# A gate table laid out by expert blocks in DRAM, five row buffers, and block 0's expert rows fetched after block 1's

## The chip, the cores and the metric

The kernel runs on one core of one Trainium2 chip. The metric is the device time of one execution in microseconds (us). The core has five engines with a program each: TensorE (PE in the profile; its weight loads are shown as PEld), VectorE (DVE), ScalarE (ACT), GpSimd (POOL) and SyncE (SP). Each works through its own program in order and waits on semaphores for the others. Sixteen DMA engines serve the transfers that SP, ACT and POOL issue.

## The reference, cut to what matters

One decoder layer on 512 tokens of width 1024: attention in sixteen heads, then a PEER feed-forward layer, in which every token picks 16 of 16384 single-neuron experts for each of 8 heads. All the work that the change touches is in the second half:

```python
def peer_ffn(xn, wq, subkeys, u_table, v_table):       # u_table, v_table: (16384, 1024)
    q = (xc @ wq).reshape(PEER_CHUNK, PEER_HEADS, 2, PEER_HALF)
    s = jnp.einsum('chpd,hpkd->chpk', q, subkeys)
    s1, i1 = lax.top_k(s[:, :, 0], PEER_TOPK)          # 16 of 128 keys
    s2, i2 = lax.top_k(s[:, :, 1], PEER_TOPK)
    cs, ci = lax.top_k(cand, PEER_TOPK)                # cand: the 256 sums s1 + s2
    eidx = jnp.take_along_axis(cidx, ci, axis=-1)      # cidx: i1 * 128 + i2
    g = jax.nn.softmax(cs, axis=-1)
    ug = jnp.take(u_table, eidx, axis=0)
    vg = jnp.take(v_table, eidx, axis=0)
    hid = jnp.einsum('cd,chkd->chk', xc, ug)
    a = jax.nn.gelu(hid, approximate=False) * g
    return jnp.einsum('chk,chkd->cd', a, vg)
```

## The kernel before, in words

The 512 tokens are four blocks of 128 (TB = 4, P = 128). The kernel handles the experts of these blocks in two ways.

**Block 0 and the first 32 tokens of block 1 fetch rows.** `gathers()` goes through 256 slots: 128 picks of block 0 from the table u, then the same picks from v. `issue(n)` takes a buffer `row` from the pool `rowp` and has POOL fetch one row of 4 KB for each of the 128 partitions (L504). For u, DVE forms the dot product of the rows with the tokens (L513, called a dot below); for v it adds the rows times their weights to `acc` (L520). `gatherq()` does the same for the first 32 tokens of block 1, spread over the 128 partitions, in 32 slots of u alone (fetch L723, dot L731). Both take their buffers from `rowp`, and a fetch into a buffer waits for the DVE instruction that used what was in it.

**The other 352 tokens (DH) are computed densely.** For each of 64 pairs of expert blocks (NPAIR; a pair is 256 experts), TensorE multiplies a 1 MB piece of u (`wraw`, split by ACT and DVE into a high part `whi` and a low part `wlo`, L126 and L127) with all 352 tokens, and ACT applies the Gelu (L534). The first 34 pairs (SPILL) are done early, and their results (`hs`) are parked in DRAM (`Hd`); the other 30 are done in the last stage. There, each pair's hidden values `ga` are multiplied on DVE (L863) by the gate table `gt`, split into `ah` (ACT, L126) and `al` (DVE, L127), and multiplied on TensorE with a 1 MB piece of v (`vr`, split into `vh` and `vl`) into six PSUM accumulators (`oa`, L886).

**The gate table** holds for each expert and token the weight of that pick, mostly zero. It is built between these two, from one-hot matrices (DVE writes `o` and `og` at L768 to L774, TensorE multiplies them into `pg`, L796; ACT copies `pg` into `gs`, L786), in 12 groups of 32 tokens (NG = 12, GT = 32), and stored in the DRAM tensor `Gd` (L788, 2 MB for each group). It is read back as `gt` in pieces of two pairs (four expert blocks, 768 KB, L835).

So there are three stages that matter here. The stage of the tables (about 480 to 780 us) interleaves table building, parked pairs (`spill`) and row fetches: `merge` mixes generators of the program by their weights, and a scheduler then orders each engine's instructions. The last stage (about 800 to 1575 us) interleaves `dense()` with `gathers()`; DVE's order there is the order of the program. Between them the gate table must have landed in `Gd` before the first `gt` can be read. In the lines of the profile `row<-in_u_dram,eq` is a fetch for block 1, and `eidx` marks one for block 0.

In the kernel before, two slots of `gathers()` (D_GATHER = 2) are taken into the stage of the tables. The generator keeps three fetches ahead of the slot that it is at, and `rowp` has four buffers.

Of the kernel before, what the change touches and what calls it, by code (L numbers as in the profile page):

```python
# [10 lines left out]
F32 = mybir.dt.float32  # L11
# [6 lines left out]
ALU = mybir.AluOpType  # L18
# [3 lines left out]
P = 128  # L22
T = 512
D = 1024
# [6 lines left out]
HK = NHEAD * TOPK  # L31
NKEY = 128
DT = T - P
GT = 32
# [8 lines left out]
NB = 8  # L43
NG = DT // GT
GS = 2.0 ** 15
NPAIR = NKEY // 2
ET = mybir.EngineType
HP = 100
GF = 1.01
SPILL = 34  # L50
D0_SPILL = 4
D1_SPILL = 4
RF = 1.04
RAWB = 2
HB = 3
SLOPES = [2.0 ** (-8.0 * (h + 1) / NH) for h in range(NH)]
D_GATHER = 2
CA, CB = 4, 12
NCAND = CA * TOPK + CB * 4

# [1 line left out]
def merge(*streams):  # L62

    live = [[0.0, total, gen] for gen, total in streams]
    while live:
        s = min(live, key=lambda e: e[0] / e[1])
        try:
            s[0] += next(s[2])
        except StopIteration:
            live.remove(s)  # L70
# [3 lines left out]
def tile_kernel(ctx: ExitStack, tc: tile.TileContext, x, w_in, w_f, b_f, w_out, wq, skT, u, v, uT, g1, g2, g2r, gfr,  # L74
                cident, ciota, ciota16, cmask, cdist, cmult, csel, out):
    nc = tc.nc

    def pool(name, bufs=1, space=None, stack=ctx):
        kw = {"space": space} if space is not None else {}
        return stack.enter_context(tc.tile_pool(name=name, bufs=bufs, reuse_waits="tile", **kw))  # L80

    gdram = pool("gdram", space=bass.MemoryType.DRAM)
    Gd = gdram.tile([NG, P, NKEY * GT], F32, name="Gd")
    hres = gdram.tile([T, D], F32, name="hres")
    xqd = gdram.tile([GT, D], F32, name="xqd")
    Hd = [gdram.tile([P, 2, DH], F32, name=f"Hd{n}") for n in range(SPILL)]
# [143 lines left out]
    while fresh or stored:  # L230
        n = fresh.pop(0) if fresh and (not stored or (nf - len(fresh)) * ns <= (ns - len(stored)) * nf) else stored.pop(0)
# [3 lines left out]
    with ExitStack() as st:  # L235
# [14 lines left out]
        with ExitStack() as s1:  # L250
# [16 lines left out]
            feed = Feed(wst, items)  # L267
# [3 lines left out]
            for b0 in range(0, TB, 2):  # L271
                nc.scalar.activation(junk[0], xs[b0 // 2][:, 0, :], AF.Square, accum_out=ss[:, b0:b0 + 1])
                sums = nc.vector.tensor_tensor_reduce(out=junk[1], in0=xs[b0 // 2][:, 1, :], in1=xs[b0 // 2][:, 1, :], scale=1.0, scalar=0.0,
                                               op0=ALU.mult, op1=ALU.add, accum_out=ss[:, b0 + 1:b0 + 2])
                _, _, norm1 = normed(xt, xp, xs[b0 // 2], b0, ss[:, b0:b0 + 2], g1c, "n1", feed.start if b0 else None)
# [182 lines left out]
        for c in range(D // WC):  # L458
# [4 lines left out]
            for b in range(0, TB, 2):  # L463
# [9 lines left out]
                if c == D // WC - 1:  # L473
                    ss = small.tile([P, 2], F32, name="n2ss")
                    nc.vector.tensor_reduce(ss, sq[:, b:b + 2, :], axis=AX.X, op=ALU.add)
                    rs, norm2, _ = normed(xt, hp, hb, b, ss, g2t, "n2")
# [8 lines left out]
            nc.sync.dma_start(hres[2 * b * P:2 * (b + 1) * P, :].rearrange("(b p) d -> p b d", p=P), h2[b])  # L485


    rowp = pool("rowp", bufs=4)
    accp = pool("accp")
    acc = accp.tile([P, D], F32, name="acc")  # L490
    hid0 = accp.tile([P, HK], F32, name="hid0")
    a0 = accp.tile([P, HK], F32, name="a0")
    nc.gpsimd.memset(acc, 0.0)


    def gathers():
        rows = {}
        slots = [(u, k) for k in range(HK)] + [(v, k) for k in range(HK)]

        def issue(n):  # L500
            if n < len(slots):
                tab, k = slots[n]
                rows[n] = rowp.tile([P, D], F32, name="row")
                nc.gpsimd.indirect_dma_start(out=rows[n], out_offset=None, in_=tab,  # L504
                                             in_offset=bass.IndirectOffsetOnAxis(ap=eidx[:, k:k + 1], axis=0))

        for n in range(3):
            issue(n)
        for n, (tab, k) in enumerate(slots):
            issue(n + 3)  # L510
            t = rows.pop(n)
            if tab is u:
                nc.vector.tensor_tensor_reduce(out=t, in0=t, in1=xn0, scale=1.0, scalar=0.0, op0=ALU.mult,  # L513
                                               op1=ALU.add, accum_out=hid0[:, k:k + 1])
                if k % TOPK == TOPK - 1:
                    sl = slice(k - TOPK + 1, k + 1)
                    nc.scalar.activation(a0[:, sl], hid0[:, sl], AF.Gelu)
                    nc.vector.tensor_mul(a0[:, sl], a0[:, sl], g0[:, sl])
            else:
                nc.vector.scalar_tensor_tensor(acc, t, a0[:, k:k + 1], acc, op0=ALU.mult, op1=ALU.add)  # L520
            yield 1.0

    def take(gen, n):
        for _ in range(n):
            try:
                yield next(gen)
            except StopIteration:
                return


    def hidden(uu, c, out_):
# [4 lines left out]
    with ExitStack() as st:  # L536
# [5 lines left out]
        NS = P // GT  # L542
# [11 lines left out]
        def spill(fd, n0, n1):  # L554
            for n in range(n0, n1):
                uu = fd.get()
                hs = hsp.tile([P, 2, DH], F32, name="hs")
                for c in range(2):
                    hidden(uu, c, hs[:, c, :])
                    yield 1.0  # L560
                nc.scalar.dma_start(Hd[n], hs)
# [54 lines left out]
        with ExitStack() as s2:  # L616
# [99 lines left out]
            def gatherq():  # L716

                rows = {}

                def issue(k):  # L720
                    if k < HK // NS:
                        rows[k] = rowp.tile([P, D], F32, name="row")
                        nc.gpsimd.indirect_dma_start(out=rows[k], out_offset=None, in_=u,  # L723
                                                     in_offset=bass.IndirectOffsetOnAxis(ap=eq4[:, k:k + 1], axis=0))

                for k in range(3):
                    issue(k)
                for k in range(HK // NS):
                    issue(k + 3)
                    t = rows.pop(k)  # L730
                    nc.vector.tensor_tensor_reduce(out=t, in0=t, in1=xnq, scale=1.0, scalar=0.0, op0=ALU.mult,  # L731
                                                   op1=ALU.add, accum_out=hq4[:, k:k + 1])
                    yield 1.0
# [22 lines left out]
            tab, work = {}, []  # L756
# [21 lines left out]
            def advance():  # L778
                if len(work) > 2 or (work and work[0][4]):
                    tok, scale, _, _, pgs, _ = work.pop(0)  # L780
                    g = tok // GT
                    if tok % GT == 0:
                        tab[g] = gsp.tile([P, NKEY, GT], F32, name="gs")
                    for n, pg in enumerate(pgs):
                        q0 = tok % GT + 4 * n
                        nc.scalar.activation(tab[g][:, :, q0:q0 + 4].rearrange("p i t -> p t i"), pg, AF.Copy, scale=scale)  # L786
                    if tok % GT == GT - NB:
                        nc.sync.dma_start(Gd[g], tab.pop(g).rearrange("p i t -> p (i t)"))  # L788
                for w in work[:-1] if len(work) > 1 else work:
                    if w[4] is None:  # L790
                        w[4] = []
                        for t4 in range(0, NB, 4):
                            pg = pgt.tile([P, 4, NKEY], F32, name="pg")
                            for tt in range(4):
                                for n in range(w[5]):
                                    nc.tensor.matmul(pg[:, tt, :], w[2][:, t4 + tt, :], w[3][n][:, t4 + tt, :], start=(n == 0), stop=(n == w[5] - 1))  # L796
                            w[4].append(pg)
                yield 2.8

            def gates3():  # L800
                yield from tables(1)
                for b in range(2, TB):
                    yield from pairs(b)
                    yield from tables(b)
                yield from tableq()
                while work:
                    yield from advance()

            L2 = 12.8 + 4.0 + 1.5 + 7.4
            merge((pairs(0), L2), (spill(feed, 0, D0_SPILL), 2.0 * D0_SPILL))  # L810
            n1 = D0_SPILL + D1_SPILL
            merge((pairs(1), L2 + 2.0), (spill(feed, D0_SPILL, n1), 2.0 * D1_SPILL))

            ga = gathers()
            merge((gates3(), RF * (2 * L2 + 7.0 + 3 * 2.8 * P // NB)), (spill(feed, n1, SPILL), 2.0 * (SPILL - n1)), (gatherq(), 1.2 * HK / NS),
                  (take(ga, D_GATHER), float(D_GATHER)))

    with ExitStack() as st:
        ep = pool("ep", bufs=2, stack=st)
# [8 lines left out]
        def load_v(i):  # L828
            if i < NPAIR:
                n = seq[i]  # L830
                raws[i] = vr = vrp.tile([P, 2, D], F32, name="vr")
                nc.sync.dma_start(vr, v[2 * n * P:2 * (n + 1) * P, :].rearrange("(c p) d -> p c d", p=P))
                if i % 2 == 0:
                    gt = gtp.tile([P, NG, 4, GT], F32, name="gt")
                    nc.sync.dma_start(gt.rearrange("p g c t -> p g (c t)"),  # L835
                                      Gd[:, :, 2 * n * GT:(2 * n + 4) * GT].rearrange("g p f -> p g f"))
                    gts[i] = gt[:, :, 0:2, :]
                    gts[i + 1] = gt[:, :, 2:4, :]
                gas[i] = ep.tile([P, 2, DH], F32, name="ga")
                if n < SPILL:  # L840
                    nc.sync.dma_start(gas[i], Hd[n])
# [46 lines left out]
                            yield 1.0  # L888

        with tc.manual_schedule(engines={ET.DVE}):  # L890
            merge((dense(), 2.0 * (NPAIR - SPILL) + 2.0 * NPAIR), (ga, GF * (2.0 * HK - D_GATHER)))


        warm(AF.Sqrt, one)
# [105 lines left out]
```

## Time and profile before

| | |
|---|---|
| runs | 1591.81, 1597.4, 1596.06 us (median 1596.06) |
| profiled execution | 1597.15 us, its span 1595.4 us |
| busy: PE, PEld, DVE, ACT, POOL | 1494.6, 1312.5, 1241.5, 646.3, 417.0 us |
| granted TensorE clock, mean over the span | 0.979 |
| moved by DMA | 400.21 MB |

The span is cut into what each engine does. "Busy" is the time in which an engine has an instruction under way; a matmul's end is modelled, so a PE that is always busy need not be at its peak. Idle time of an engine is put down to whatever ended it. The granted clock is the share of full speed at which TensorE was let run.

### The profile page before, as it was taken

To read this page: it belongs to the slowest core of one execution; us is meant where nothing else is said; L and a number is where in the kernel's file an instruction comes from. 1 tells how busy PE (TensorE), PEld (TensorE's weight loads), DVE (VectorE), ACT (ScalarE), POOL (GpSimd) and SP (SyncE) were. 2 spreads that over 40 slices of the span, in tenths; PEclk is the share of its full clock that TensorE was granted. 3 is DMA by queue.
4 is the path that set the end of the run, shared out by engine and by line. 5 is a ranking of instruction groups with operands and counts; after the bars stand their busy time and mean duration, and the time that the engine had idled before them with its cause. 6 is when DMAs were issued, how large, how long until landed. Compare 5 with 4: busy or idle time off the path is not lost. (4 is left out here: it accounts for less than half of the span.)

```text
span 1595.4 us, 22534 instructions
## 1 busy us (share of the span) xinstructions
PE 1494.6 (94%) x8722; PEld 1312.5 (82%) x8722; DVE 1241.5 (78%) x2336; ACT 646.3 (41%) x811; POOL 417.0 (26%) x306
## 2 busy tenths in 40 slices
PE   7999999999988989889899999999899999999996
PEld 6787888988887878878878787888788888888885
DVE  7455565579998889888687787877778887888877
ACT  6455554422344637556533233332233333333323
POOL 2000000000002142110034344435444444344441
PEclk9999999999999999999999999999999999999998
DMA  5212112422246877857999999989899999999985
GB/s 191 80 53 80 53 54 95 148 94 91 106 170 221 315 247 267 313 202 289 331 362 350 344 322 339 347 311 367 304 334 353 356 341 341 347 324 364 321 314 191
DMA packets 145979, 400.21 MB, mean 251 GB/s; under 512 B 10192, under 2 KB 59600, under 8 KB 141136
## 3 DMA queue, kind: packets, MB, share of 16 engines
q1 hardware_dynamic: 97264, 231.69, 41.3%
q0 software_dynamic: 42272, 151.74, 25.7%
q10 hardware_dynamic: 6336, 15.35, 2.6%
q8 instruction: 68, 1.11, 0.3%
q14 instruction: 39, 0.32, 0.1%
HBM read 357.45 MB, written 41.75 MB: 250 GB/s over the span
## 5 line engine op out<-in xcount | busy, mean ns | idle before, releaser
L155 PE MATMUL pj<-xh,whi 128*128 128x352 f32 (+2 forms) x1304 | 446.8, 343 | 21.4 <-ACT hs L534 15.0
L155 PE MATMUL pj<-xh,wlo 128*128 128x352 f32 (+2 forms) x1304 | 444.4, 341 | 5.1 <-DVE wlo L127 5.1
L155 PE MATMUL pj<-xl,whi 128*128 128x352 f32 (+2 forms) x1304 | 444.7, 341 | 0.0
L155 PEld LDWEIGHTS pj<-xh,whi 128*128 128x128 f32 x1304 | 249.9, 192 | 36.2 <-ACT hs L534 16.9
L886 PE MATMUL oa<-vh,ah 128*128 128x512 f32 x768 | 243.3, 398 | 25.6 <-ACT ah L126 25.4
L126 ACT ACTIVATE whi<-wraw 128x2048 fp32r<-128x2048 f32 (+1 forms) x89 | 169.8, 1908 | 234.3 <-PE pj L155 207.9
L155 PEld LDWEIGHTS pj<-xh,wlo 128*128 128x128 f32 x1304 | 250.0, 192 | 16.6 <-DVE wlo L127 6.8
L155 PEld LDWEIGHTS pj<-xl,whi 128*128 128x128 f32 x1304 | 250.2, 192 | 10.0
L504 POOL DMA_INDIRECT row<-in_u_dram,eidx x128 | 177.1, 1384 | 294.8 <-DVE hid L513 247.6
L886 PE MATMUL oa<-vh,al 128*128 128x512 f32 x768 | 243.2, 397 | 3.9 <-DVE al L127 3.9
L127 DVE TENSOR_TENSOR wlo<-wraw,whi 128x2048 fp32r<-128x2048 f32 (+1 forms) x89 | 202.4, 2275 | 53.2 <-ACT whi L126 53.2
L886 PE MATMUL oa<-vl,ah 128*128 128x512 f32 x768 | 240.4, 394 | 0.0
L504 POOL DMA_INDIRECT row<-in_v_dram,eidx x128 | 176.9, 1382 | 212.3 <-DVE acc L520 181.0
L886 PEld LDWEIGHTS oa<-vh,ah 128*128 128x128 f32 x768 | 144.1, 191 | 60.7 <-ACT ah L126 33.4
L513 DVE CUSTOM_DVE_ANT_0 row<-row,xn 128x1024 f32<-128x1024 f32 x128 | 152.4, 1220 | 49.7 <-DMA row<-in_u_dram,eidx 49.4
L520 DVE SCALAR_TENSOR_TENSOR acc<-row,a,acc 128x1024 f32<-128x1024 f32 x128 | 164.2, 1283 | 33.5 <-DMA row<-in_v_dram,eidx 31.2
L886 PEld LDWEIGHTS oa<-vh,al 128*128 128x128 f32 x768 | 144.5, 191 | 42.0 <-DVE al L127 12.9
L886 PEld LDWEIGHTS oa<-vl,ah 128*128 128x128 f32 x768 | 146.3, 190 | 31.1
L126 ACT ACTIVATE vh<-vr 128x2048 fp32r<-128x2048 f32 x64 | 122.3, 1913 | 111.4 <-DMA vr<-in_v_dram 96.8
L126 ACT ACTIVATE ah<-gt 128x768 fp32r<-128x768 f32 x64 | 54.1, 845 | 271.7 <-DVE gt L863 263.9
L723 POOL DMA_INDIRECT row<-in_u_dram,eq x32 | 53.3, 1667 | 405.5 <-ACT hs L534 237.4
L127 DVE TENSOR_TENSOR vl<-vr,vh 128x2048 fp32r<-128x2048 f32 x64 | 146.2, 2284 | 7.4 <-ACT vh L126 7.4
(227 smaller groups left out, 1742.4 us busy)
## 6 DMA issues: line engine op xcount, KB each, us to landing
wraw<-in_uT_dram SPq DMA_DIRECT2D x64, 1024.0 KB
vr<-in_v_dram SPq DMA_DIRECT2D x64, 1024.0 KB
Gd<-gs SPq DMA_DIRECT2D x12, 2048.0 KB
gt<-Gd SPq DMA_DIRECT2D x32, 768.0 KB
wraw<-in_w_in_dram SPq DMA_DIRECT2D x12, 1024.0 KB
Hd<-hs ACTq DMA_DIRECT2D x34, 352.0 KB
ga<-Hd SPq DMA_DIRECT2D x34, 352.0 KB
wraw<-in_wq_dram SPq DMA_DIRECT2D x8, 1024.0 KB
```

The lines of the kernel that those rows point to most:

```text
L126: nc.scalar.activation(hi, src, AF.Copy)
L127: nc.vector.tensor_sub(lo, src, hi.bitcast(F32))
L155: nc.tensor.matmul(ps, a, c, start=(i == 0), stop=(i == 3 * n - 1))
L504: nc.gpsimd.indirect_dma_start(out=rows[n], out_offset=None, in_=tab, in_offset=bass.IndirectOffsetOnAxis(ap=eidx[:, k:k + 1], axis=0))
L513: nc.vector.tensor_tensor_reduce(out=t, in0=t, in1=xn0, scale=1.0, scalar=0.0, op0=ALU.mult, op1=ALU.add, accum_out=hid0[:, k:k + 1])
L520: nc.vector.scalar_tensor_tensor(acc, t, a0[:, k:k + 1], acc, op0=ALU.mult, op1=ALU.add)
L723: nc.gpsimd.indirect_dma_start(out=rows[k], out_offset=None, in_=u, in_offset=bass.IndirectOffsetOnAxis(ap=eq4[:, k:k + 1], axis=0))
L886: nc.tensor.matmul(oacc[b][d], w[:, c, sl], m[:, c, d * 512:(d + 1) * 512], start=s0, stop=s1)
```

## The change

- The table in DRAM gets the order [32 blocks of four expert blocks][128 partitions][12 token groups][4 x 32 values]. Before it was [12 groups][128 partitions][128 expert blocks x 32 values].
- A store of a group (L788 before) now writes, for each partition, 32 pieces of 512 B; it wrote one piece of 16 KB. A read of `gt` (L835 before) now takes one piece of 6 KB for each partition; it took 12 pieces of 512 B.
- `rowp` has five buffers, and both row generators keep four fetches ahead.
- `gathers()` no longer takes part in the stage of the tables. Its first four fetches are issued behind the last of `gatherq()`, and all its 256 slots are used up in the last stage.
- The accumulator `acc` moves from a place of its own to memory that the stage of the tables has used, and is cleared when this is free; five row buffers and the rest then fit.

```diff
+ROWB = 5
-D_GATHER = 2
-    Gd = gdram.tile([NG, P, NKEY * GT], F32, name="Gd")
+    Gd = gdram.tile([NPAIR // 2, P, NG, 4 * GT], F32, name="Gd")
-    rowp = pool("rowp", bufs=4)
+    rowp = pool("rowp", bufs=ROWB)
     accp = pool("accp")
-    acc = accp.tile([P, D], F32, name="acc")
-    nc.gpsimd.memset(acc, 0.0)
+    accs = []
...
-        for n in range(3):
+        for n in range(ROWB - 1):
             issue(n)
+        yield 0.0
         for n, (tab, k) in enumerate(slots):
-            issue(n + 3)
+            issue(n + ROWB - 1)
...
-                for k in range(3):
+                for k in range(ROWB - 1):
                     issue(k)
                 for k in range(HK // NS):
-                    issue(k + 3)
+                    issue(k + ROWB - 1)
...
-                        nc.sync.dma_start(Gd[g], tab.pop(g).rearrange("p i t -> p (i t)"))
+                        nc.sync.dma_start(Gd[:, :, g, :].rearrange("n p f -> p n f"), tab.pop(g).rearrange("p (n c) t -> p n (c t)", c=4))
...
+            merge((gates3(), RF * (2 * L2 + 7.0 + 3 * 2.8 * P // NB)), (spill(feed, n1, SPILL), 2.0 * (SPILL - n1)), (gatherq(), 1.2 * HK / NS))
             ga = gathers()
-            merge((gates3(), RF * (2 * L2 + 7.0 + 3 * 2.8 * P // NB)), (spill(feed, n1, SPILL), 2.0 * (SPILL - n1)), (gatherq(), 1.2 * HK / NS),
-                  (take(ga, D_GATHER), float(D_GATHER)))
+            next(ga)
+
+    acc = pool("accq").tile([P, D], F32, name="acc")
+    nc.gpsimd.memset(acc, 0.0)
+    accs.append(acc)
...
-                    nc.sync.dma_start(gt.rearrange("p g c t -> p g (c t)"),
-                                      Gd[:, :, 2 * n * GT:(2 * n + 4) * GT].rearrange("g p f -> p g f"))
+                    nc.sync.dma_start(gt.rearrange("p g c t -> p (g c t)"), Gd[n // 2].rearrange("p g f -> p (g f)"))
...
-            merge((dense(), 2.0 * (NPAIR - SPILL) + 2.0 * NPAIR), (ga, GF * (2.0 * HK - D_GATHER)))
+            merge((dense(), 2.0 * (NPAIR - SPILL) + 2.0 * NPAIR), (ga, GF * 2.0 * HK))
```

On POOL, the program from the stage of the tables to the end, before (`eq` marks the fetches for block 1, `eidx` those for block 0):

```order
L493 MEMSET acc 128x1024
L549 MEMSET aq 128x128
L723 DMA row<-in_u_dram,eq_3190 128x1024 x4
L504 DMA row<-in_u_dram,eidx 128x1024 x4
L723 DMA row<-in_u_dram,eq_3190 128x1024 x19
L504 DMA row<-in_u_dram,eidx 128x1024
L723 DMA row<-in_u_dram,eq_3190 128x1024 x9
L504 DMA row<-in_u_dram,eidx 128x1024 x123
L504 DMA row<-in_v_dram,eidx 128x1024 x128
```

And the same stretch of POOL's program now:

```order
L543 MEMSET aq 128x128
L717 DMA row<-in_u_dram,eq_3188 128x1024 x32
L504 DMA row<-in_u_dram,eidx 128x1024 x5
L813 MEMSET acc 128x1024
L504 DMA row<-in_u_dram,eidx 128x1024 x123
L504 DMA row<-in_v_dram,eidx 128x1024 x128
```

The five fetches of block 0 that stood among those of block 1 now stand behind them all, and the clearing of `acc` stands behind those five.

On DVE, at the start of the stage of the tables, before (`og` and `o` are the one-hot matrices, `hq` and `hid` the results of the dots of block 1 and block 0):

```order
L731 ISA row,hq_3191<-row,xnq 128x1024
L731 ISA hq_3191 128x1
L774 TENSOR_TENSOR og<-o_4957,tg_4872 128x1024
L513 ISA row,hid_3172<-row,xn_105 128x1024
L513 ISA hid_3172 128x1
L774 TENSOR_TENSOR og<-o_4957,tg_4872 128x1024
L768 TENSOR_TENSOR o_5012<-iota,tri 128x1024
```

And at that place now:

```order
L725 ISA row,hq_3189<-row,xnq 128x1024
L725 ISA hq_3189 128x1
L768 TENSOR_TENSOR og<-o_4948,tg_4870 128x1024 x2
L762 TENSOR_TENSOR o_5003<-iota,tri 128x1024
```

The dot of block 0 is gone from between the two `og`; the dots of block 1 stay spread among the table work. A second dot of block 0 is gone farther on in the same stage, and both are now done in the last stage.

On SP, the end of the stage of the tables, before:

```order
L189 DMA wraw<-in_uT_dram 128x2x1024 x2
L832 DMA vr<-in_v_dram 128x2x1024
L788 DMA Gd<-gs 128x4096
L832 DMA vr<-in_v_dram 128x2x1024
L835 DMA gt<-Gd 128x12x128
```

And now:

```order
L189 DMA wraw<-in_uT_dram 128x2x1024 x2
L830 DMA vr<-in_v_dram 128x2x1024
L782 DMA Gd<-gs 128x32x128
L830 DMA vr<-in_v_dram 128x2x1024
L833 DMA gt<-Gd 128x1536
```

The order on SP is the same here; what changed is the shape of the store (32 pieces for each partition) and of the read (one piece).

## Rows read from the trace of the kernel before

**Rows 1.** Windows: length, then each engine's busy us; clock, DMA share, GB/s.
```profile
480.00:780.00 300.00, 266.84 (x2041) 249.23 (x2041) 262.17 (x486) 171.82 (x190) 59.79 (x38) 0.95 0.75 269
...
800.00:1570.00 770.00, 743.16 (x3604) 639.10 (x3602) 617.57 (x658) 245.65 (x218) 343.95 (x247) 0.99 0.93 336
```

**Rows 2.** Waits from 480 to 780 us: who waited for whom, total, times, longest.
```profile
POOL row L723 <- DVE hq L731: 140.3, 23, 11.3
...
DVE row L731 <- DMA row<-in_u_dram,eq: 25.1, 12, 6.1
PE pg L796 <- DVE og L774: 16.4, 9, 3.3
...
ACT whi L126 <- DMA wraw<-in_uT_dram: 12.9, 3, 6.6
...
PE pj L155 <- ACT hs L534: 9.1, 3, 4.6
```

**Rows 3.** Timeline, 555 to 600 us: start, us, instruction, idle before and its releaser.
```profile
564.56 1.22 DVE L731 CUSTOM_DVE_ANT_0 row<-row,xnq 128x1024 f32<-128x1024 f32 x1 [6.07 <-DMA row<-in_u_dram,eq]
...
566.27 0.31 ACT L653 ACTIVATE ex<-ex 128x128 f32<-128x128 f32 x1 [5.70 <-DVE ex L639]
...
568.50 0.43 PE L155 MATMUL pj<-xh,whi 128*128 128x352 f32 x1 [3.76 <-ACT hs L534]
```

**Rows 4.** Timeline of POOL and DVE in the stage of the tables, 522 to 531 us.
```profile
522.53 1.15 POOL L723 DMA_INDIRECT row<-in_u_dram,eq  x1 [9.60 <-DVE hq L731]
...
529.25 1.23 DVE L731 CUSTOM_DVE_ANT_0 row<-row,xnq 128x1024 f32<-128x1024 f32 x1 [3.38 <-DMA row<-in_u_dram,eq]
```

**Rows 5.** Waits from 860 to 1570 us.
```profile
ACT vh L126 <- DMA vr<-in_v_dram: 80.0, 24, 7.0
...
DVE row L513 <- DMA row<-in_u_dram,eidx: 46.9, 22, 4.1
...
DVE acc L520 <- DMA row<-in_v_dram,eidx: 31.2, 22, 3.4
...
PE oa L886 <- ACT ah L126: 21.2, 9, 5.2
```

**Rows 6.** Timeline of one stall in the last stage, 865 to 882 us.
```profile
867.44 1.68 POOL L504 DMA_INDIRECT row<-in_u_dram,eidx  x1 [5.11 <-DVE hid L513]
869.43 3.05 POOL L504 DMA_INDIRECT row<-in_u_dram,eidx  x1 [0.30 <-issue]
...
877.96 1.23 DVE L513 CUSTOM_DVE_ANT_0 row<-row,xn 128x1024 f32<-128x1024 f32 x1 [4.01 <-DMA row<-in_u_dram,eidx]
...
881.00 1.22 PE L886 MATMUL oa<-vh,ah 128*128 128x512 f32 x2 [5.06 <-ACT ah L126]
```

**Rows 7.** Timeline of PE: three more stalls of the last stage.
```profile
983.61 0.73 PE L886 MATMUL oa<-vh,ah 128*128 128x512 f32 x2 [2.64 <-ACT ah L126]
...
1139.22 1.22 PE L886 MATMUL oa<-vh,ah 128*128 128x512 f32 x2 [5.15 <-ACT ah L126]
...
1358.50 1.22 PE L886 MATMUL oa<-vh,ah 128*128 128x512 f32 x2 [3.71 <-ACT ah L126]
```

**Rows 8.** DMA from 900 to 1500 us: queue, packets, MB, share of 16 engines; issues.
```profile
q1 hardware_dynamic: 60160, 102.34, 49.1%
q0 software_dynamic: 27775, 101.12, 44.5%
...
gt<-Gd SPq DMA_DIRECT2D x23, 768.0 KB
```

**Rows 9.** DMA from 500 to 780 us.
```profile
q1 hardware_dynamic: 8384, 49.29, 48.2%
...
Gd<-gs SPq DMA_DIRECT2D x12, 2048.0 KB
```

**Rows 10.** Timeline of SP and ACT between the stages, 787 to 791 us.
```profile
787.24 0.37 SPq L835 DMA_DIRECT2D gt<-Gd  x1
...
790.28 0.46 ACT L534 ACTIVATE ga<-pj 128x352 f32<-128x352 f32 x1 [8.32 <-DMA Hd<-hs]
```

More of the change, by code (lines that the diff above doesn't have):

```diff
@@ L519, in gathers @@
             else:
-                nc.vector.scalar_tensor_tensor(acc, t, a0[:, k:k + 1], acc, op0=ALU.mult, op1=ALU.add)
+                nc.vector.scalar_tensor_tensor(accs[0], t, a0[:, k:k + 1], accs[0], op0=ALU.mult, op1=ALU.add)
             yield 1.0
[L523 to L528, printed above, removed]
     def hidden(uu, c, out_):
```

## Prediction

> **What bounds the kernel now.** I read the windows first, in two long stretches, then the waits of each, then the timeline at the longest waits of TensorE, and last the DMA queues. Two stages hold what the change touches [rows 1]. In the stage of the tables, 480 to 780 us, PE is busy for 266.8 of 300 us at a granted clock of 0.95: 33.2 us of idle time, and some 5% of 267 us, about 13 us, given up to the clock (0.95 is a mean over its two levels, 2.4 and 1.2 GHz, so the lower one held for about a tenth of the stage). In the last stage, 800 to 1570 us, PE is busy for 743.2 of 770 us at 0.99: 26.8 us idle, and about 7.7 us by the clock. So TensorE sets the pace, and the change can only win what TensorE loses: at most 46 us in the first of these stages and 35 us in the second.
>
> What ends TensorE's waits is VectorE, mostly at one remove. In the stage of the tables TensorE waits for the one-hot matrices of DVE (16.4 us) and for a PSUM buffer that ACT empties (9.1 us) [rows 2]. DVE itself waits 25.1 us there, twelve times, for rows of block 1, so it is working or waiting for rows in 287 of 300 us. The timeline shows how such a wait travels: DVE stands 6.07 us for a row, the exponent on ACT behind it waits 5.70 us, ACT is late for the PSUM buffer that stands behind that, and TensorE idles 3.76 us [rows 3]. Why the rows are late is seen in the fetches: 23 times POOL waits for a dot of block 1 to free a buffer, 140.3 us in all [rows 2]. Three of the four buffers hold rows of block 0 at that time (four were fetched, two dots are taken, each followed by one more fetch), so one buffer circulates: a fetch goes out at 522.53 only when the dot before it has ended, and its dot at 529.25 has waited 3.38 us [rows 4].
>
> In the last stage DVE waits 46.9 + 31.2 = 78.1 us for rows, 44 times, and TensorE waits 21.2 us for `ah`, nine times [rows 5]. At the longest of these, DVE stands 4.01 us for a row, the gate product behind it is late by that, and PE idles 5.06 us [rows 6]. Three more stalls have the same end, 2.64, 5.15 and 3.71 us [rows 7], and in the timeline DVE stands for a row just ahead of each. That is 16.6 us of PE idle time behind four waits for rows.
>
> **The change part by part.** *Fetches of block 1 by themselves.* With no rows of block 0 in the pool, five buffers serve block 1, and four fetches are ahead of each dot. The dots stay spread over the stage: 32 in 300 us, one in 9 us. One fetch took 6.7 us to land (522.53 to 529.25 [rows 4]), and now it goes out some four dots, over 30 us, before its dot. I expect all of the 25.1 us to go but the first waits of the stage, 3 us in two, and with them the two waits of block 0's dots there; 24 us less on DVE in all. How much of that reaches TensorE is bounded by nothing and by all of it; the one chain that I followed gave 3.76 for 6.07, and TensorE has other waits in between. I take half: **-12 us**. The two dots that leave the stage (1.22 us each, as all dots [rows 6]) come back in the last one: 2.5 us there and back, 0 in the sum.
>
> *One more buffer in the last stage.* A row is fetched when the dot five before it is done, where it was four. In the stall above, the row for 877.96 was fetched at 869.43, and POOL needed 3.05 us for it; now it takes the place of the fetch at 867.44, which was through at 869.12, 3.4 us before the other. Of 4.01 us of waiting some 0.6 would be left. Against that, four fetches in flight instead of three share the same DMA engines, so each is slower. I take 70% of what hangs on these waits: the 16.6 us and two thirds of the clock loss, 5 us, together 21.6 us, and 70% of it is **-15 us**. The bounds are 0 and all 35 us.
>
> *Reads of `gt` in one piece.* From 900 to 1500 us queue q0, whose pieces are rows of 4 KB, moved 101.12 MB in 44.5% of the time, 379 GB/s while busy [rows 8]. Queue q1 moved 102.34 MB in 49.1% of it, 347 GB/s. If its other 84.2 MB went at q0's rate (222 us), the 23 reads of `gt`, 18.1 MB in pieces of 512 B, took 72 us, or 250 GB/s; in large pieces they would take 48. Over all 32 reads that is 34 us of DMA time saved, in a stage whose DMA share is 0.93 [rows 1]. It is DMA time, not TensorE's. It shortens the waits for `vr` (80.0 us on ACT [rows 5]), of which little shows on PE: what is left of the 26.8 us when the four stalls are taken off is 10 us. I take **-3 us**, between 0 and -10.
>
> *Stores of `Gd` in 32 pieces.* No store in pieces of 512 B is in the trace, so its price is bounded. The lower bound is the present rate of q1 in this stage, 49.29 MB in 48.2% of 280 us, 365 GB/s [rows 9]: twelve stores of 2 MB are 25.2 MB, 69 us, and the change costs nothing. The nearest row in size of piece is the read above at 250 GB/s: 101 us, 32 us more, 2.7 us for each store. I take this. The DMA share of the stage goes from 0.75 to 0.86, so the DMA engines are not full. But loads of `wraw` queue behind the stores on SP: ACT waits for them three times now, 12.9 us [rows 2]. With one late load for four stores, a quarter of the 32 us is seen by ACT, and half of this by TensorE as above: **+4 us**, between 0 and all 32.
>
> The Trainium skill (DMA: Bandwidth & Descriptors, "Why small descriptors are slow (HBM only)") gives a fixed overhead of about 3 cycles to each piece beside one cycle for 32 bytes; by this a piece of 512 B costs 16% more per byte than one of 4 KB (19/16 against 131/128), an estimate. The trace's 250 against 379 GB/s is 52% more, so sign and order agree and the size doesn't. With the page's figure the twelve stores would take 11 us more instead of 32, the term would be +1 or +2 instead of +4, and the sum 1568 us.
>
> *Between the stages.* ACT waits 8.32 us there for the store of `Hd` before it can write `ga` into memory that this store reads, and `gt` is issued at 787.24, when the last group has landed [rows 10]. The store of that group gets 2.7 us longer, and `gt` is read faster by (72 - 48)/23, some 1 us; TensorE has two pairs of u to work on meanwhile. I take 0, between -4 and +5. Clearing `acc` now waits on POOL for the last stores of `Hd`, with fetches behind it; but five rows of block 0 have been fetched ahead of it, and the sixth is wanted only when five dots are done. It costs nothing unless those stores land 10 us later than now.
>
> The sum: -12 - 15 - 3 + 4 = -26 us against the profiled execution, whose time was 1597.15 us, span 1595.4 us and 1.8 us around it. That gives 1571 us. The median of the runs shown is 1 us below this execution, which is inside their spread of 5.6 us.
>
> **The rivals.** *Both stages reach TensorE's floor.* If DVE's waits for rows go and nothing follows them, idle time and clock losses can shrink together: the stage with 11% of idle time had a granted clock of 0.95, that with 3.5% had 0.99 [rows 1]. For it: DVE is the only engine that works or waits for rows nearly all the time. Against it: 10 us of the last stage's idle time and half of the other's have other ends. Two thirds of the 46 and 35 us would give 1543 us.
>
> *The rows wait elsewhere.* In the last stage the DMA engines are busy for 93% of the time, and four fetches in flight can wait as long in the engines as three did in the pool; ACT then waits for `vr`. In the stage of the tables TensorE may find the next late thing (the loads of `wraw`, the serial selection on DVE). Then a few us remain and the stores eat them: 1597 us. For it: q0 and q1 share the same engines. Against it: moving less per stage is not needed, only earlier, and the stage of the tables has a quarter of its DMA time free.
>
> *The stores bind the stage of the tables (slower).* 25% of 300 us, 75 us, of DMA time is free there, and the stores take 69 us now. At 144 us for them, 175 GB/s, the engines are full; every us above lengthens the stage. To cancel the 30 us won elsewhere, the stores would have to take 174 us, 145 GB/s. At half the price of the read, 125 GB/s, they take 202 us, 58 us too many: 1597 - 30 + 58 = 1625 us. For it: one store has 4096 pieces, the read 1536, and the pieces of a partition lie 768 KB apart in DRAM. Against it: the reads now have pieces as small, and go at 250 GB/s.
>
> **How the numbers follow.** Chances: the forecast 0.63, the floor 0.12, rows waiting elsewhere 0.15, the stores binding 0.10. About 0.3% (5 us) is what a measurement of this kernel can tell from no change. The forecast's own range is 1560 to 1584. For the whole, the lower end reaches towards the floor, -44 us, and the upper end to the rows waiting elsewhere: 1553 to 1595; half of the floor's cases and those of the stores lie outside. Faster: the forecast, the floor and a third of the second rival, 0.80. Same: half of the second rival, 0.08. Slower: the rest, 0.12.
>
> **What would show it.** In the stage of the tables DVE's waits for rows of block 1 fall from 25.1 us to about 3, POOL no longer waits 140 us for dots of one buffer at a time, and the clock rises above 0.95. In the last stage the 78.1 us fall to about 25, and PE stalls of over 2.5 us behind `ah` are gone or down to one. The DMA share of q1 in the last stage falls by some 4 points at equal traffic, and it rises in the stage of the tables by about 11; ACT waits for `wraw` some 20 us there. The prediction is wrong if these waits go and TensorE's idle time stays, or if the stores take 12 us and more each.

## The result, and the profile after

The changed kernel takes 1530.08 us (median of four runs, 1528.18 to 1531.73) against 1596.73 us for the kernel before (four runs, 1591.81 to 1603.74): a ratio of 0.9579, 95% interval 0.9541 to 0.9617. Its profiled execution took 1531.73 us with a span of 1530.0 us. The gain of some 67 us is two and a half times the 26 us that I predicted, and far below the low end of the range.

The first read of `gt` parts the two stages well in every kernel here. It was issued at 787.24 us before [rows 10] and at 770.25 us after. Cut there, the windows of the kernel before read (columns as in [rows 1]):

```profile
480.00:787.20 307.20, 273.52 (x2082) 255.62 (x2081) 267.72 (x492) 173.77 (x191) 61.47 (x39) 0.95 0.75 270
787.20:1595.40 808.20, 765.34 (x3696) 658.26 (x3696) 638.59 (x709) 262.23 (x248) 345.83 (x249) 0.98 0.92 332
```

and those of the changed kernel:

```profile
480.00:770.20 290.20, 271.43 (x2100) 254.64 (x2099) 264.62 (x489) 175.05 (x194) 52.11 (x38) 0.97 0.85 288
770.20:1530.00 759.80, 744.45 (x3685) 650.39 (x3684) 640.02 (x711) 261.57 (x247) 362.23 (x252) 1.00 0.94 353
```

The stage of the tables lost 17.0 us and the last stage, with its end, 48.4. In the last stage PE's idle time went from 42.9 us (808.20 - 765.34) to 15.4, which is 27.5 us; nearly the same matmuls (3685 records, 3696 before) kept it busy for 20.9 us less, at a clock of 1.00 where it was 0.98. So nearly half of what was won there goes with the clock.

The waits of the stage of the tables answer to [rows 2]:

```profile
POOL row L717 <- DVE hq L725: 117.1, 20, 23.6
...
ACT whi L126 <- DMA wraw<-in_uT_dram: 25.8, 5, 8.1
...
PE pj L155 <- ACT hs L528: 9.9, 4, 3.3
...
PE pg L790 <- DVE og L768: 5.0, 4, 2.4
...
DVE row L725 <- DMA row<-in_u_dram,eq: 3.2, 2, 2.4
```

DVE's waits for rows of block 1 fell from 25.1 to 3.2 us, and TensorE's for `og` from 16.4 to 5.0. POOL still waits 117.1 us for dots: it has nothing else to do, and a buffer that comes free late no longer means a row that lands late. ACT's waits for `wraw` doubled, from 12.9 us; they are 18.3 us with the two other edits alone, so 7.5 of the 25.8 come with the new stores.

The waits of the last stage, 843 to 1505 us, answer to [rows 5]:

```profile
ACT vh L126 <- DMA vr<-in_v_dram: 42.7, 11, 7.5
...
DVE acc L521 <- DMA row<-in_v_dram,eidx: 4.8, 5, 1.9
DVE row L514 <- DMA row<-in_u_dram,eidx: 4.0, 5, 1.9
...
PE oa L883 <- ACT ah L126: 1.9, 2, 1.5
```

The 78.1 us in which DVE waited for rows are 8.8, and no stall of TensorE behind `ah` longer than 1.5 us is left in this stretch. The DMA queues there, 850 to 1450 us (beside [rows 8]):

```profile
q1 hardware_dynamic: 27823, 108.03, 48.3%
q0 software_dynamic: 30037, 109.35, 47.8%
```

Both queues together are at 96%, where they were at 94%, and still TensorE's own waits in the last stage fell from 33.4 to 5.2 us in all. Queue q1 now moves 373 GB/s while busy (108.03 MB in 48.3% of 600 us), where it moved 347; its pieces have grown, 27823 packets for 108 MB against 60160 for 102.

Between the stages:

```profile
764.70 0.46 ACT L528 ACTIVATE ga<-pj 128x352 f32<-128x352 f32 x1 [1.70 <-PE pj L155]
...
770.25 0.34 SPq L833 DMA_DIRECT2D gt<-Gd  x1
...
770.16 0.95 POOL L813 MEMSET acc<- 128x1024 f32 x1 [53.44 <-DMA Hd<-hs]
...
771.27 0.94 POOL L504 DMA_INDIRECT row<-in_u_dram,eidx  x1 [0.15 <-issue]
```

The first `ga` no longer waits 8.32 us for a store of `Hd`. Clearing `acc` stood on POOL for 53 us and held nothing up: DVE's first wait for a row of block 0 comes at 837 us and lasts 0.78 us:

```profile
837.86 1.23 DVE L514 CUSTOM_DVE_ANT_0 row<-row,xn 128x1024 f32<-128x1024 f32 x1 [0.78 <-DMA row<-in_u_dram,eidx]
```

### The profile page after: what moved, and what is told of

Same layout as the page of the kernel before. It is cut to its first block, busy times and chain, and to the rows that moved or that the text cites. A ratio compares the mean times of both kernels' runs of the same rounds, so it can differ in the third digit from the quotient of the medians.

```text
span 1530.0 us, 22523 instructions
## 1 busy us (share of the span) xinstructions
PE 1474.1 (96%) x8722; PEld 1306.7 (85%) x8722; DVE 1239.6 (81%) x2336; ACT 647.0 (42%) x811; POOL 423.0 (28%) x306
## 5 line engine op out<-in xcount | busy, mean ns | idle before, releaser
L155 PE MATMUL pj<-xh,whi 128*128 128x352 f32 (+2 forms) x1304 | 447.0, 343 | 18.3 <-ACT hs L528 15.1
L504 POOL DMA_INDIRECT row<-in_u_dram,eidx x128 | 187.5, 1465 | 209.3 <-DVE hid L514 154.1
L883 PE MATMUL oa<-vh,ah 128*128 128x512 f32 x768 | 237.5, 390 | 3.8 <-ACT ah L126 3.8
L883 PE MATMUL oa<-vh,al 128*128 128x512 f32 x768 | 237.9, 390 | 0.6 <-DVE al L127 0.5
L504 POOL DMA_INDIRECT row<-in_v_dram,eidx x128 | 180.3, 1409 | 186.3 <-DVE acc L521 155.1
L883 PEld LDWEIGHTS oa<-vh,al 128*128 128x128 f32 x768 | 143.8, 188 | 32.3 <-DVE al L127 2.4
L717 POOL DMA_INDIRECT row<-in_u_dram,eq x32 | 45.5, 1423 | 385.4 <-DMA wraw<-in_uT_dram 237.4
L127 DVE TENSOR_TENSOR al<-gt,ah 128x768 fp32r<-128x768 f32 x64 | 61.3, 958 | 64.3 <-ACT ah L126 64.3
```

The costliest lines, as they stand in the source:

```text
L127: nc.vector.tensor_sub(lo, src, hi.bitcast(F32))
L155: nc.tensor.matmul(ps, a, c, start=(i == 0), stop=(i == 3 * n - 1))
L883: nc.tensor.matmul(oacc[b][d], w[:, c, sl], m[:, c, d * 512:(d + 1) * 512], start=s0, stop=s1)
```

## The experiments

The theory that I formed on the result, W, is that the waits of DVE for rows are the whole of it, and that each us of them costs TensorE nearly a us, in idle time and in clock. The rivals gave a larger part to the layout (faster reads of `gt`, D: the DMA engines), or to something that only the three edits together bring. The expectations use P for the point that, in the stage of the tables, DVE's own time is what the stage lasts. The table holds the kernels that take the change apart, and four more follow below; `layout_only`, `order_only`, `buffers_only` and `all_but_...` are the labels of those named alike here. Its stages are those of the profiled execution, cut at the first read of `gt`, and the waits are over the span. Each ratio is to the kernel before as it was timed beside that run (medians from 1594.72 to 1596.73 us). A stage is read from one execution, and executions of one kernel differ by up to 16 us (13 of the kernel before: 1583.20 to 1599.04), so a few us between two stages can be chance.

| kernel | median us | ratio [95%] | start of last stage | last stage | DVE waits for rows u / v / block 1 | PE waits for `ah` |
|---|---|---|---|---|---|---|
| before | 1596.73 | | 787.2 | 808.2 | 49.4 / 31.2 / 25.1 | 25.4 |
| after | 1530.08 | 0.9579 [0.9541, 0.9617] | 770.2 | 759.8 | 4.8 / 4.8 / 3.2 | 3.8 |
| layout alone | 1584.84 | 0.9944 [0.9917, 0.9971] | 788.8 | 789.6 | 46.6 / 24.5 / 23.3 | 17.9 |
| order alone | 1571.70 | 0.9856 [0.9802, 0.9911] | 760.4 | 811.0 | 46.1 / 32.3 / 1.8 | 31.1 |
| buffers alone | 1541.74 | 0.9672 [0.9618, 0.9726] | 777.7 | 761.1 | 10.8 / 6.4 / 18.3 | 6.3 |
| all but the layout | 1527.76 | 0.9580 [0.9527, 0.9633] | 759.7 | 766.9 | 12.3 / 5.6 / 3.7 | 7.7 |
| all but the order | 1546.02 | 0.9697 [0.9668, 0.9727] | 783.3 | 760.7 | 7.8 / 4.4 / 18.1 | 8.1 |
| all but the buffers | 1562.24 | 0.9805 [0.9770, 0.9839] | 765.4 | 792.3 | 46.1 / 26.7 / 2.3 | 19.0 |
| order, three buffers | 1654.65 | 1.0397 [1.0355, 1.0439] | 761.1 | 886.7 | 89.4 / 73.2 / 4.3 | 88.6 |
| five buffers, three ahead | 1537.61 | 0.9652 [0.9620, 0.9684] | 770.6 | 761.3 | 13.0 / 5.3 / 7.6 | 6.8 |

**The layout alone, and all but the layout.** On the kernel before, or back on the kernel after:

```diff
-    Gd = gdram.tile([NG, P, NKEY * GT], F32, name="Gd")
+    Gd = gdram.tile([NPAIR // 2, P, NG, 4 * GT], F32, name="Gd")
```

with the store and the read of `gt` that go with it, as in the diff of the change.

> The kernel before with the new layout of the gate table alone (stores in 32 pieces, gt read in one piece; four buffers, three fetches ahead, block 0 among block 1). Theory W (what counts is how many row buffers are free ahead of a dot): DVE's waits for rows stay near 78 us in the last stage and 25 us in the stage of the tables, and the time moves by -3 to +4 us against before, 1590 to 1600. Theory D (what counts is the DMA time that gt's reads of 512 B take, since rows queue behind them): DVE's waits for rows in the last stage fall to under 40 us, and the time falls by 20 to 40 us, 1557 to 1577.

> The changed kernel with the old layout of the gate table (five buffers, four fetches ahead, block 0 behind block 1). Theory W: nearly the whole gain, 1530 to 1537, and DVE's waits for rows in the last stage at most 20 us. Theory D: 1550 to 1575, with DVE's waits for rows in the last stage over 40 us and the DMA share there at 0.97 or more.

Alone the layout wins 10 us by the medians, between what W and what D had said, and all of it in the last stage (808.2 to 789.6 us, in an execution that lies 5 us under its median). DVE's waits for rows stay, as W had it: 71.1 us, where they were 80.6. These 9.5 us seem to be only a part of what that stage gained, so W may be too narrow here; ACT's waits for `vr` fell by 28.7 us (96.8 to 68.1), and their part in it isn't shown. On top of the two other edits the layout wins nothing: 1530.08 with it, 1527.76 without, in intervals that overlap. It pays only while buffers are few.

**The order alone.** On the kernel before, four buffers and three ahead:

```diff
         for n in range(3):
             issue(n)
+        yield 0.0
...
-                  (take(ga, D_GATHER), float(D_GATHER)))
+            next(ga)
```

with `ga` made behind the merge, and its weight GF * 2.0 * HK.

> The kernel before with block 0's fetches behind block 1's alone (four buffers, three fetches ahead, old layout). Both theories: DVE's waits for rows of block 1 in the stage of the tables fall from 25 us to under 8, and this stage gets 10 to 20 us shorter. Theory W: the last stage keeps DVE's waits for rows of about 78 us and its length, so 1576 to 1588 in all. A third theory (the last stage's waits come from how it starts, with how many rows in flight) would shorten the last stage too, under 1570.

Its windows:

```profile
480.00:760.40 280.40, 263.66 (x2091) 246.04 (x2089) 266.06 (x491) 173.13 (x191) 52.31 (x38) 0.99 0.81 294
760.40:1571.40 811.00, 763.76 (x3696) 657.23 (x3696) 640.54 (x711) 261.62 (x248) 343.00 (x251) 0.98 0.92 332
```

The stage of the tables is 26.8 us shorter, more than the 10 to 20 expected, for 23.3 us less of DVE's waits (25.1 to 1.8), and its clock is 0.99 where it was 0.95; so the whole, 1571.70 us, lies below W's range. The last stage is no shorter, and the third theory falls: it is 2.8 us longer, about the two dots of 1.22 us that it took over, though 2.8 us can also be chance. The first stage's 266.1 us of DVE work now lie in 280.4 us, so little room is left; a kernel with more work on DVE, below, tests this.

**The buffers alone.** On the kernel before: five buffers, four fetches ahead, `acc` in its later place.

```diff
-    rowp = pool("rowp", bufs=4)
+    rowp = pool("rowp", bufs=5)
...
-            issue(n + 3)
+            issue(n + 4)
```

> The kernel before with five row buffers and four fetches ahead alone (acc moved as in the change; old layout, block 0 still among block 1, two dots of it in the stage of the tables). Theory W: the last stage gains what all_but_layout gains there (40 us or more), and the stage of the tables gains less than the change does, since four of five buffers hold rows of block 0 there and one circulates as before: DVE's waits for rows of block 1 stay at 20 to 25 us, in all 1545 to 1555. Theory D: the last stage gains 10 us or less, 1580 to 1592.

```profile
480.00:777.70 297.70, 272.24 (x2101) 254.16 (x2100) 266.44 (x493) 177.48 (x195) 52.33 (x40) 0.96 0.79 281
777.70:1538.80 761.10, 743.90 (x3679) 650.76 (x3677) 638.03 (x707) 261.24 (x245) 354.62 (x249) 0.99 0.96 352
```

The last stage falls to 761.1 us, that of the whole change, and DVE's waits for rows of block 0 from 80.6 to 17.2 us. The edit also moves `acc` and fetches one farther ahead. The move is not the cause, since with `acc` moved and four buffers (all but the buffers) 72.8 us of waits stay; the distance is tested below. So this one buffer carries most of the result. It gives the stage of the tables 9.5 us besides, which W did not expect, and DVE's waits there fall to 18.3 us although one buffer circulates as before; why isn't shown.

**All but one, for the other two.** The kernel after with `ROWB = 4`, and `buffers_only` with the layout added.

> The changed kernel with four row buffers and three fetches ahead (block 0 behind block 1, new layout). Theory W: the stage of the tables as after (first read of gt at 760 to 772 us), the last stage as order_only's or a little shorter for the reads of gt, DVE's waits for rows there 65 to 80 us; 1560 to 1575 in all. Theory D: DVE's waits under 40 us and 1540 or less.

> The changed kernel with block 0's fetches still among block 1's (five buffers, four ahead, new layout, two dots of block 0 in the stage of the tables). If the parts add up as the runs so far suggest: the last stage as after (about 760 us from the first read of gt), the stage of the tables as buffers_only's or up to 10 us longer for the stores; 1540 to 1555 in all, DVE's waits for rows of block 1 15 to 25 us.

Both came out as expected. By medians the buffer is worth 53 us alone and 32 us as the last edit to come; the order 23 and 16; the layout 10 and -2 (alone against 1595.03 us, the kernel before beside these three runs). The parts overlap: the buffer takes some of what the order wins in the stage of the tables, and what the layout wins in the last one. The layout's share goes with the number of buffers: about 10 us won with four (1571.70 to 1562.24 with the order), and none with five, where the 2 to 4 us lost (1527.76 to 1530.08, 1541.74 to 1546.02) are within the noise.

**Three buffers.** All but the layout, with `ROWB = 3`.

> all_but_layout with three row buffers and two fetches ahead. Theory W (the last stage waits for rows as long as too few are under way): DVE's waits for rows in the last stage rise from 18 us with five buffers and 78 with four to over 200, and the last stage is longer than with four buffers by 80 us or more, over 1640 in all. Theory D (the DMA engines' share sets it): the share falls and the time stays within 20 us of order_only's 1572.

```profile
DVE row L514 <- DMA row<-in_u_dram,eidx: 89.4, 41, 5.2
PE oa L884 <- ACT ah L126: 88.6, 19, 8.2
DVE acc L521 <- DMA row<-in_v_dram,eidx: 73.2, 41, 4.5
```

The time went the way of W, and waits and stage fell a little short of its "over 200" and "80 us or more". With order and layout alike (the kernel with four has `acc` in its old place), three, four and five buffers give last stages of 886.7, 811.0 and 766.9 us, and DVE's waits for rows there are 162.6, 78.4 and 17.9 us. From three to four, 84.2 us of waits are worth 75.7 us; from four to five, 60.5 are worth 44.1: 0.90 and 0.73 us for each us. The stage of the tables doesn't care, 761.1, 760.4 and 759.7 us, since with the order a single generator of rows has all the buffers.

**Five buffers, three ahead.** The kernel `buffers_only` with the distance of before.

```diff
-            issue(n + 4)
+            issue(n + 3)
```

> buffers_only with the fetches three ahead of the slot in the program as before, not four; five buffers. POOL's program holds the fetches alone, in the same order either way, so what lets one start is a free buffer. If so, the time and DVE's waits are those of buffers_only, 1538 to 1546. If the distance in the program counts, they are those of before, about 1595, or between.

The time is about what was expected (1537.61 us), and the last stage is the same, 761.3 us. The waits for rows of block 1 are not: in the stage of the tables three of the five buffers are now held by block 0, not four, so two circulate, and DVE waits 7.6 us instead of 18.3. So the free buffers count, not how far ahead the program writes its fetches.

**More work on DVE in the stage of the tables.** All but the layout, with every third one-hot `o` written a second time; nothing is left out.

```diff
+                if (tok // NB) % 3 == 0:
+                    nc.vector.tensor_tensor(pairs_of(o2), ib, tri[:, 1, ts_, None, :].to_broadcast(pair), ALU.is_equal)
```

> all_but_layout with every third one-hot matrix o (L762) written twice on DVE: 16 more instructions of 0.69 us, 11.0 us, in the stage of the tables; nothing else changes, and the second write repeats the first. Theory P (DVE sets the pace of this stage, so its time counts in full): all_but_layout + 9 to 12 us, 1537 to 1540. Theory H (a half of DVE's time reaches the end, as the prediction had it): + 4 to 6 us, 1532 to 1534.

The stage of the tables with it, 1539.13 us in all (ratio 0.9662 [0.963, 0.9694]):

```profile
480.00:769.20 289.20, 271.50 (x2115) 254.60 (x2114) 273.67 (x505) 177.96 (x195) 51.41 (x41) 0.98 0.79 288
```

and without it (the kernel all but the layout):

```profile
480.00:759.70 279.70, 262.50 (x2076) 245.59 (x2075) 263.01 (x489) 173.84 (x192) 50.73 (x37) 0.98 0.81 296
```

DVE is busy for 10.7 us more, the stage lasts 9.5 us longer and the median is 11.4 us higher: P, not H. In this stage, with the order changed, DVE's time is nearly the stage's time, which fits with waits that counted in full in `order_only`.

**The table's pitch.** The kernel before with 4 KiB behind each group's 2 MiB, so that the 12 pieces of a read of `gt` lie 2 MiB + 4 KiB apart.

```diff
-    Gd = gdram.tile([NG, P, NKEY * GT], F32, name="Gd")
+    Gd = gdram.tile([NG, P * NKEY * GT + 1024], F32, name="Gd")
```

> The kernel before with the twelve groups of the gate table 2 MiB + 4 KiB apart in DRAM instead of 2 MiB; pieces stay 512 B. If the price of the reads (250 GB/s while busy) is one of the pitch, queue q1 rises in the last stage from 347 to about 373 GB/s, as with the new layout, and the time falls as far as layout_only's, by some 9 us. If it is one of the piece's size, q1 stays at 345 to 350 GB/s and the time within 5 us of before.

Neither: 1659.75 us, a ratio of 1.042 [1.0385, 1.0455]. The stage of the tables is as before (it ends at 783.9 us); the last one lasts 873.9 us, 65.7 more. Its waits:

```profile
DVE row L513 <- DMA row<-in_u_dram,eidx: 80.8, 26, 6.7
PE oa L886 <- ACT ah L126: 73.9, 19, 11.2
DVE acc L520 <- DMA row<-in_v_dram,eidx: 67.9, 26, 5.7
```

They are hardly more frequent than in the kernel before, 26 for each table where [rows 5] have 22, but longer: 148.7 us over the span instead of 80.6. These 68.1 us more stand beside 65.7 us more of stage, so here too the price comes by way of late rows. The reads of `gt` take from issue to landing, 900 to 1450 us:

```profile
DMA to landing us min/median/max: 7.0/9.5/12.5
```

In the kernel with three buffers, whose reads have the same pieces 2 MiB apart and whose DMA share is the same (0.87), they take:

```profile
DMA to landing us min/median/max: 5.5/6.9/9.1
```

Two more kernels ask whether this is the address or the new form of the access: the same flat form without padding, and with 512 bytes of it.

```diff
-    Gd = gdram.tile([NG, P * NKEY * GT + 1024], F32, name="Gd")
+    Gd = gdram.tile([NG, P * NKEY * GT], F32, name="Gd")
```

> The kernel before, with the table in DRAM declared as [NG, P*NKEY*GT] without the 1024 elements of padding, stored and read through the same flat views as in padded_pitch; every byte stands where it stands in the kernel before, and every engine's rows are those of before. Theory A (the address: tables that start 2 MiB + 4 KiB apart are slower to read than tables 2 MiB apart): 1590 to 1600 us, a ratio within 0.4% of 1, gt reads landing faster than the median 9.5 us of padded_pitch by 2 us or more. Theory V (the view: the flat access pattern is cut into other pieces, whatever the addresses): 1645 to 1670 us as padded_pitch had, gt reads landing after 9 us or more.

> As padded_pitch (1659.75 us), but with 128 elements (512 bytes) of padding behind each token group's table in place of 1024 (4 KiB). Theory A in its narrow form (a step of 4 KiB puts the pieces of one read onto the same part of the memory, and 512 bytes spreads them): within 0.5% of before, or faster by up to 0.6% as layout_only was. Theory A in its wide form (any step that isn't 2 MiB loses something that the aligned tables have): 1630 to 1670 us. Theory V (the view): 1645 to 1670 us.

1593.28 us (ratio 0.9992 [0.9972, 1.0011]) and 1588.55 us (0.9968 [0.9947, 0.999]): the form costs nothing and 512 bytes cost nothing. (The traces of these two hold no landing times.) It is the address, with a step of 2 MiB + 4 KiB, that costs 65 us. The padding may also move the DRAM tensors declared behind `Gd`; of these `Hd` is read in the last stage, and its reads land no later (a median of 6.7 us, 6.9 with three buffers). Why reads of `gt` that land 2.6 us later make rows late isn't settled: other transfers land later too (`vr` after a median of 9.2 us, 7.2 with three buffers; rows after 7.8 and up to 14.0 us, 6.5 and 10.0 there), but what the reads collide with in memory no view shows.

## Why the prediction was wrong

**The mechanism was right, and the sizes were too small by far.** Rows arrived late because buffers came free late; the change mends this in both stages, and the waits that I named went. The sum gave -8 for the stage of the tables (-12 and +4) and -18 for the last one (-15 and -3). The spans show -17.0 and -48.4.

**"I take half" (the order, -12 us).** DVE works or waits for rows in 287 of 300 us there: I had this number and still halved its waits. In `order_only` the stage lost 26.8 us for 23.3 us of waits, and the kernel with more work on DVE agrees: nearly all that is added to DVE there comes out at the end. So the halving is the error, and its reason, other waits of TensorE in between, did not hold. The clock is part of this: 0.95 to 0.99. With five buffers the order is worth less, 18.0 us in this stage, since the buffers had taken 9.5 already.

**"70% of what hangs on these waits" (one more buffer, -15 us).** This step failed most: the last stage lost 47.1 us in `buffers_only`. That the fetches would slow each other was right (they land after a median of 7.3 us with four buffers and 7.9 with five, order and layout alike), but it cost little. Three parts of the step were wrong. First, I let DVE's 78.1 us of waits fall to 25, and they fell to 8.8 (17.2 over the span of `buffers_only`). Second, I hung 16.6 us of TensorE's idle time on them, the four long stalls, and gave the other 10 of the 26.8 us to "other ends". In `buffers_only` the stretch that answers to mine, from 12.8 us behind the first read of `gt` to 25.4 us before the end, reads

```profile
790.50:1513.40 722.90, 721.65 (x3579) 632.20 (x3578) 614.98 (x657) 247.25 (x217) 350.80 (x246) 1.00 0.98 358
```

which leaves 1.3 us of idle time: with the buffer alone nearly all of it went, short waits too. Third, I priced the clock at 7.7 us from a mean of 0.99 and called 35 us the bound. PE's busy time over the last stage fell by 21.4 us in `buffers_only` as the clock rose. A mean with two digits, times 770 us, is uncertain by 4 us either way, and the window that I cut left out the first 13 us behind the tables and the end, with which it reads 0.98. The bound that I took for the stage was itself too small.

**Reads of `gt` in one piece (-3 us).** The price in DMA time was about right: q1 went to 373 GB/s, where I had set 379 for large pieces, and it was busy for 28 us less over the last stage (48.3% of 808.2 us, then 47.7% of 759.8), where I had 34. Its effect depends on the buffers: with four, the last stage lost 18.6 us (`layout_only`) and 18.7 (`all_but_buffers` against `order_only`); with five, 7.1 and 0.4. I had let only ACT's waits for `vr` shorten; with four buffers DVE's waits for rows shrink too, by 9.5 and 5.6 us. How the rest of the gain comes about stays open.

**Stores in 32 pieces (+4 us).** The sign was right. In the stage of the tables, 480 to 763 us:

```profile
q1 hardware_dynamic: 53237, 51.72, 55.7%
```

That is 157.6 us of the engines; at the rate of before [rows 9], 365 GB/s, these 51.72 MB take 141.7. Twelve stores cost 16 us more, 1.3 us each and about 296 GB/s, half of the 2.7 us that I took. The stage is longer by 1.6 us (layout alone), 5.0 (on top of the order), 5.6 (of the buffers) and 10.5 (of both), one execution each, so the +4 came out about right. That was luck: the DMA time was half of mine, and the way that I gave for it isn't shown, since ACT's waits for `wraw` rose by 8.0, 14.4, 4.9 and 7.5 us in these pairs, out of step with the stage. By the Trainium skill (DMA: Bandwidth & Descriptors, "Why small descriptors are slow (HBM only)") I had estimated 16% per byte for such pieces; the stores show 23% (365 against 296 GB/s) and the reads of before 52%, so sign and order agree, and of the sizes that of the stores is the nearer. The 52% was never measured by itself: it rests on the share of q1 that I gave to `gt`.

**Between the stages (0).** ACT's 8.32 us for `Hd` went with the old place of `acc`: in all the kernels of the table that have `acc` moved, the first `ga` starts within 2 us of the issue of the last store of `Hd`, and in the three others it waits 7 to 8 us for that store. I had not seen this coming. TensorE's wait for the first `ga` fell from 4.1 to 0.9 us: -3, inside my bounds. Clearing `acc` was free, as I had it.

**The rivals.** The floor (1543 us) was nearest, but it took two thirds of two bounds, and the last stage alone lost 48.4 us, more than all of its 35. That rows would wait in the DMA engines fell: their share rose to 0.96, and yet DVE's waits for rows went and ACT's waits for `vr` halved (80.0 to 42.7 us). The stores didn't bind: the DMA share of the tables' stage is 0.85.

**What I said would show it** held: 25.1 to 3.2 us, clock 0.97, stalls behind `ah` gone, q1's share down by 3 points at equal traffic (48.3% for 108.03 MB is 45.8% for the 102.34 of before), up by 9 in the stage of the tables (47.0, for 480 to 780 us, to 55.7), ACT's waits for `wraw` at 25.8 us. The 78.1 us went farther than I said, to 8.8 and not 25. Only POOL's 140 us stayed (117), while DVE's waits went, so they were not the cost.

## What to carry to other kernels

Where an engine is working or waiting in nearly all of a stage, as DVE in the stage of the tables, expect its waits to count in full. In the last stage, where DVE is not always busy and TensorE follows it by way of ACT, each us of them was still worth 0.73 to 0.96 us: don't discount them by the number of long stalls that the bottleneck engine shows. Count the buffers of a random fetch that are really free, since here one of them was worth more than the faster transfers, and these were worth something only while buffers were short. Take what the clock gives back from the busy time of equal matmuls in a good and a bad stretch, not from a rounded mean.

## What the runs showed of the hardware

A step of 2 MiB + 4 KiB between the pieces of a read costs this kernel 4.2%, where 2 MiB and 2 MiB + 512 bytes cost nothing. The Trainium skill (DMA: Bandwidth & Descriptors, "Latency and other measured facts") advises to pad row pitches at large powers of two by a few KiB, and reports that, in copies from DRAM to DRAM, 4 KiB brought the full rate back where the rows of the partitions lay 4 MiB apart. Here the partitions lie 16 KiB apart and only the 12 groups 2 MiB, and the padding did harm; in such a shape it has to be measured.

DMA engines that are busy for 96% of a stage aren't yet a bound. With three, four and five buffers, order and layout alike, the DMA share of the last stage is 0.87, 0.92 and 0.96, fetches of rows land after a median of 6.5, 7.3 and 7.9 us, and the stage lasts 886.7, 811.0 and 766.9 us: each fetch takes longer, but with more of them under way DVE waits less.
